# A fifth chunk of the exponentials off ScalarE, at pair 46, with the products on VectorE, and new orders of every engine, in a cosine-similarity attention kernel

## The chip, the cores and the metric

The kernel runs on one core of one Trainium2 chip. The metric is the device time of one execution in microseconds (us): the median over runs. A profile of one execution gives, beside its time, a trace of every instruction; "span" is the time from the first to the last instruction in that trace. Engines carry the profile's names: PE is TensorE (matmuls), PEld its weight loads, ACT ScalarE, DVE VectorE, POOL GpSimd, SP the engine that only issues transfers.

## The reference

For 8 batches of 12 heads, 512 rows of 64 numbers each:

```python
Q_norm = Q / (np.linalg.norm(Q, axis=-1, keepdims=True) + 1e-10)
K_norm = K / (np.linalg.norm(K, axis=-1, keepdims=True) + 1e-10)
scores = np.einsum('bhqd,bhkd->bhqk', Q_norm, K_norm) / tau
weights = np.exp(scores - np.max(scores, axis=-1, keepdims=True))
weights = weights / (np.sum(weights, axis=-1, keepdims=True) + 1e-10)
return np.einsum('bhqk,bhkd->bhqd', weights, V)
```

with tau = 0.1. Scores lie between -10 and 10, so the kernel subtracts no maximum.

## The kernel before, in words

**Pairs and chunks.** Two heads are a pair; there are 48 pairs, 0 to 47. The 512 keys of a pair are four chunks of 128. One chunk holds the scores of 128 keys against 512 queries for both heads: 128 x 1024 numbers. Every pair goes through the same stages, which the code names by short keys and this text uses as well:

- LD, LV (lines 340 to 344): transfers of Q, K and V from memory, issued by SP; ST (709) stores the output.
- SQ (lines 352 to 370): squares of Q and K on GpSimd. SSQ (397 to 411) and RED (382 to 424): their sums over 64 numbers, on TensorE and VectorE; for some pairs BN and RED (line 386) take Q's sums as batch statistics on VectorE.
- NEW (lines 446 to 478): the reciprocal roots of a group of up to four pairs, small steps on VectorE, held in the PSUM bank of `n_ps`. UNIT (481) rescales them for a pair that has a chunk off ScalarE.
- SCL (488 to 492): Q and K times their factors, Q on VectorE, K mostly on GpSimd. TR (497 to 505): transposes on TensorE into the bank `t_ps`. EVA (514 to 519): VectorE's copy of both transposes to SBUF.
- SCO (634 to 646): the scores of one chunk, two matmuls into one of two double banks of `sc_ps`; so a chunk's scores wait for the exponential of the chunk two before.
- EXP (654 to 662): ScalarE's exponential of a chunk, `et` in bfloat16. The last chunk of pair 47 is done in three pieces (647 to 653).
- VC (668 to 674): V cast to bfloat16 on GpSimd, mostly for two pairs at once.
- PV (678 to 694): weights times V, eight blocks of four matmuls for a pair. A column of ones beside V gives the row sums. RCP, NRM (702 to 708): reciprocal of the sums and the product, for both heads at once ("joint") or, in a pair with a chunk off ScalarE, for each head.

**A chunk off ScalarE.** `OFF` (line 755) lists chunks whose exponential is not ScalarE's: chunk 3 of pairs 26, 35, 41 and 46. `poly` (559 to 620) makes it from powers of two and a polynomial. For each head SCX puts the scores in the bank of the transposes (`x_ps` is the same memory as `t_ps`, line 157), after the copies of that pair; X0 (line 578) rounds them to an integer `xp` and X1 (580) takes the remainder `xz`, both on VectorE. Then GpSimd does five steps Y0 to Y4 over both heads (lines 600 to 607): square, scale, scale, product, product with the power of two. The blocks PV that use this chunk come last in their head and wait for Y4.

**The order of the work.** Nothing is decided at run time. Each engine executes its own list, written out in `ORDER` (lines 818 to 909) as numbers of operations in the order of `P.add`; an engine waits at an operation until all that it needs has been done, and everything behind it in its list waits as well. The lists interleave pairs: VectorE prepares pairs many places ahead of the one whose exponentials run. Decoded, VectorE's list ends, from the copy of pair 43 on (numbers are pair, head or tensor, step):

```
EVA.43 SCL.44.0 UNIT.46 SCL.45.0 SCL.46.0 EVA.44 RCP.40.0 NRM.40.0 EVA.45 EVA.46 RCP.41.0 X.46.0.0 NRM.41.0
X.46.0.1 RCP.41.1 NRM.41.1 X.46.1.0 X.46.1.1 RCP.42.0 NRM.42.0 SCL.47.0 RCP.43.0 NRM.43.0 RCP.44.0 NRM.44.0
EVA.47 RCP.45.0 NRM.45.0 RCP.46.0 RCP.46.1 NRM.46.0 NRM.46.1 RCP.47.0
...
```

GpSimd's ends `SQ.46 Y.41.0 Y.41.1 Y.41.2 Y.41.3 SCL.44.1 SCL.45.1 SCL.46.1 Y.41.4 VC.42 VC.44 VC.46 SCL.47.1 Y.46.0 Y.46.1 Y.46.2 Y.46.3 Y.46.4`.

## Time and profile before

| | us |
|---|---|
| median of 3 runs | 187.42 |
| lowest and highest run | 187.32, 188.6 |
| the profiled execution | 187.29 |
| its span | 185.3 |

How to read it: the busy time of an engine counts instructions that overlap once, so a mean duration times a count can exceed it. The chain that ended last is followed back from the last instruction, at each step to what released it; it is given as a list in order of time (start, length, what). A row of the groups has the line, engine and operation, the written and read tiles, the shape and the count, then total busy time and mean duration in ns, then the idle time of the engine in front of these instructions and who ended it. A timeline row has start, length, engine, line and operation, merged where several of a kind follow each other; an idle time in front stands in brackets. A row of waits has who waited for whom, the total, how often, and the longest.

### The profile page before, as it was taken

How to read it: one execution, taken by the hardware profiler on the slowest of the kernel's cores; microseconds unless marked ns; L12 is line 12 of the kernel's file. 1: busy time of each engine (PE TensorE's matmuls, PEld its weight loads, DVE VectorE, ACT ScalarE, POOL GpSimd, SP SyncE). 2: the span in 40 equal slices, each digit the busy share in tenths (PEclk: the TensorE clock that was granted, in tenths of full speed). 3: DMA queues.
4: the chain of work that ended last, by engine and by line, in shares of the span. 5: the costliest groups of instructions: out<-in, count | busy, mean ns of one | idle time of the engine just before them, and what ended most of it. 6: DMA issues, size and time to landing. Idle time of an engine off the chain costs nothing.

```text
span 185.3 us, 6949 instructions
## 1 busy us (share of the span) xinstructions
PE 174.9 (94%) x2802; PEld 111.4 (60%) x2802; DVE 167.6 (90%) x604; ACT 178.6 (96%) x208; POOL 162.2 (88%) x151
## 2 busy tenths in 40 slices
PE   7989999999999999999998999999899999899983
PEld 2556666666666666665664666675465656555652
DVE  2788999999999999999999999999999999989453
ACT  5799999999999999999999999999999999999993
POOL 4799989969889879696999999999899998999970
PEclk9999999999999999999999999999999999999998
DMA  5999999999999996999999996889978232211333
GB/s 172 343 351 350 350 358 339 283 340 377 379 379 382 371 372 217 278 371 355 379 363 357 381 378 217 233 263 316 357 252 265 79 117 79 96 61 57 117 113 117
DMA packets 52448, 50.79 MB, mean 274 GB/s; under 512 B 3136, under 2 KB 52416, under 8 KB 52416
## 3 DMA queue, kind: packets, MB, share of 16 engines
q1 hardware_dynamic: 51984, 50.02, 81.6%
q8 instruction: 22, 0.36, 0.8%
q10 hardware_dynamic: 432, 0.33, 0.5%
q14 instruction: 10, 0.08, 0.1%
HBM read 37.75 MB, written 12.58 MB: 272 GB/s over the span
## 4 chain that ended last, share of the span: by engine, by line
ACT 90%; PE 4%; DVE 2%; DMA 1%; issue 0%; POOL 0%; DVEq 0%
ACT et L660 89%; PE oops L685 2%; DMA qk<-in_K_dram 1%; PE scps L636 1%; DVE ob L706 1%; DVE xs L264 1%; PE oops L722 0%; DVE ob L735 0%; PE tps L287 0%; POOL sq L260 0%; ACT ys L437 0%; DVE qn L277 0%; PE scps L287 0%; DVE rd L704 0%; ACT nps L440 0%
## 5 line engine op out<-in xcount | busy, mean ns | idle before, releaser
L660 ACT ACTIVATE et<-scps 128x1024 bf16<-128x1024 f32 (+1 forms) x189 | 172.2, 1114 | 0.6 <-PE scps L636 0.5
L636 PE MATMUL scps<-qt 64*128 64x512 bf16 x376 | 73.9, 386 | 4.4 <-ACT et L660 2.8
L685 PE MATMUL oops<-vb,et 128*128 128x65 bf16 x1504 | 71.5, 194 | 0.6 <-DVE ob L706 0.3
L685 PEld LDWEIGHTS oops<-vb,et 128*128 128x128 bf16 x1504 | 54.8, 97 | 27.2 <-issue 19.3
L490 POOL TENSOR_TENSOR qn<-qk,rk 128x512 bf16<-128x512 f32 x42 | 43.3, 1043 | 8.7 <-DVE rk L448 7.2
L367 POOL TENSOR_TENSOR sq<-qk 128x512 bf16<-128x512 f32 x34 | 35.0, 1039 | 0.9 <-PE tps L499 0.8
L490 DVE TENSOR_TENSOR qn<-qk,nps 128x512 bf16<-128x512 f32 x52 | 34.4, 678 | 0.6 <-ACT nps L440 0.6
L706 DVE TENSOR_TENSOR ob<-oops,rd 128x512 f32<-128x512 f32 (+1 forms) x61 | 34.3, 563 | 0.2
L517 DVE COPY qt<-tps 128x1024 bf16<-128x1024 bf16 x47 | 32.2, 685 | 1.6 <-PE tps L499 1.1
L499 PE MATMUL tps<-ident,qn 128*128 128x128 bf16 x376 | 32.4, 220 | 1.0 <-DVE qn L490 0.6
L636 PEld LDWEIGHTS scps<-qt 64*128 64x128 bf16 x376 | 18.6, 92 | 22.0 <-ACT et L660 8.8
L386 DVE BATCH_NORM_STATS2 st<-qk 128x6 f32<-128x128 f32 x136 | 31.6, 284 | 0.0
L499 PEld LDWEIGHTS tps<-ident,qn 128*128 128x128 bf16 x376 | 21.4, 98 | 12.9 <-issue 8.0
L669 POOL TENSOR_SCALAR vb<-vf 128x1024 bf16<-128x1024 f32 (+1 forms) x29 | 25.9, 909 | 0.8 <-DMA vf<-in_V_dram 0.5
L370 POOL TENSOR_TENSOR sq<-qk 128x1024 bf16<-128x1024 f32 x10 | 18.8, 1893 | 0.3 <-DMA qk<-in_K_dram 0.3
L704 DVE RECIPROCAL rd<-oops 128x8 f32<-128x8 f32 (+1 forms) x61 | 11.6, 191 | 6.2 <-PE oops L685 5.1
L406 PE MATMUL oops<-sq,ident 128*128 128x64 bf16 x320 | 15.9, 193 | 0.0
L406 PEld LDWEIGHTS oops<-sq,ident 128*128 128x128 bf16 x320 | 12.0, 98 | 1.8 <-issue 1.4
L601 POOL TENSOR_TENSOR xw<-xw,xz 128x1024 f32<-128x1024 f32 x4 | 9.4, 2357 | 0.2
L601 POOL TENSOR_TENSOR xw<-xz 128x1024 f32<-128x1024 f32 x4 | 7.6, 1892 | 1.8 <-DVE xz L580 1.8
L601 POOL TENSOR_TENSOR et<-xw,xp 128x1024 bf16<-128x1024 f32 x4 | 8.5, 2130 | 0.2
L419 DVE TENSOR_REDUCE nps<-oops 128x8 f32<-128x64 f32 x36 | 7.4, 205 | 0.4 <-PE oops L406 0.2
(67 smaller groups left out, 102.8 us busy)
## 6 DMA issues: line engine op xcount, KB each, us to landing
vf<-in_V_dram SPq DMA_DIRECT2D x48, 256.0 KB, 6.5
qk<-in_Q_dram SPq DMA_DIRECT2D x47, 256.0 KB, 6.4
qk<-in_K_dram SPq DMA_DIRECT2D x47, 256.0 KB, 6.4
out_dram<-ob SPq DMA_DIRECT2D x47, 256.0 KB, 5.5
qk<-in_Q_dram SPq DMA_DIRECT2D x2, 128.0 KB, 2.4
qk<-in_K_dram ACTq DMA_DIRECT2D x2, 128.0 KB, 2.7
out_dram<-ob SPq DMA_DIRECT2D x1, 128.0 KB, 1.7
out_dram<-ob SPq DMA_DIRECT2D x1, 64.0 KB, 1.7
```

What stands on the lines that cost most here:

```text
L367: lambda e: e.tensor_tensor(out=sqf[:, 8 * DIM :], in0=data[:, 8 * DIM :], in1=data[:, 8 * DIM :], op=ALU.mult))
L386: last = e.bn_stats(out=st[:, g % R_X, c8 + 4 * h + t : c8 + 4 * h + t + 2, :].rearrange("p g x -> p (g x)"), in_=rows[:, t : t + 2].rearr ...
L406: last = e.matmul(out=o_ps[bank][:, at : at + 64], lhsT=ident[:, :], rhs=sq[iqs][:, 8 * w : 8 * w + 8, 8 * k : 8 * k + 8], start=(k == 0), ...
L490: lambda e, w=w, r=r: e.tensor_tensor(out=qn[iqn][:, w].rearrange("p t h d -> p h t d"), in0=qk[iq][:, w].rearrange("p h (t d) -> p h t d" ...
L499: last = e.transpose(t_ps[:, w, t, :], qn[iqn][:, w, t].rearrange("p h d -> p (h d)"), ident[:, :])
L517: lambda e, ws=ws: e.tensor_copy(out=qt[iqt][:, ws, :, :].rearrange("p w t x -> p (w t x)"), in_=t_ps[:, ws, :, :].rearrange("p w t x -> p ...
L601: mul = lambda o, x, y: lambda e: e.tensor_tensor(out=o, in0=x, in1=y, op=ALU.mult)
L636: last = e.matmul(out=sc_ps[:, 2 * b + h, :], lhsT=qt[iqt][64 * h : 64 * h + 64, 1, c, :], rhs=qt[iqt][64 * h : 64 * h + 64, 0, :, :], sta ...
L660: lambda e, c=c, b=b, hs=hs: e.activation(out=et[iet][:, c, hs[0] : hs[-1] + 1, :], in_=sc_ps[:, 2 * b + hs[0] : 2 * b + hs[-1] + 1, :], f ...
L669: return e.tensor_scalar(out=vb[:, ib // 2, :, ib % 2 : ib % 2 + n, :, 0:DIM].rearrange("p c r h d -> p (r h) c d"), in0=vf[:, iv : iv + n ...
L685: last = e.matmul(out=o_ps[h][:, 65 * t : 65 * t + 65], lhsT=et[iet][:, c, h, 128 * t : 128 * t + 128], rhs=vb[:, s % R_VB // 2, c, s % 2, ...
L706: lambda e, hs=hs, grid=grid: e.tensor_tensor(out=ob[io][:, hs], in0=grid[:, :, :, 0:DIM], in1=rd[io][:, hs, :].unsqueeze(3).to_broadcast( ...
```

## The change

Five chunks instead of four leave ScalarE: chunk 3 of pairs 25, 33, 40 and 44, done as before with five steps on GpSimd, and of pair 46, done in a new way (`IN_PSUM`). The scores of pair 46's chunk go to two banks: head 0 to the transposes' bank after the copy of pair 47 (the last that uses it), head 1 to the bank of the factors, after the scales of the last 12 pairs (`SCL`), when nothing uses it any more. X0 and X1 write tiles of their own (`yp`, `yz`). Then, for each head, VectorE makes the first product (Y1: `yz` and `yp`, both in SBUF, into the PSUM bank), GpSimd squares `yz` in place (Y2, after both Y1), and VectorE makes the second product (Y3: `yz` and the bank, into `et`). Y1 also waits for the last GpSimd step of pair 44. A constant factor that the products leave out is put into the other three chunks of pair 46: their exponentials get a bias, a tile of 128 x 1 that GpSimd sets once. The blocks PV of pair 46's chunk wait for Y3 of their own head alone. Pairs 26, 35 and 41 get joint normalisations; 25, 33, 40 and 44 get one for each head. `NRM_ON_POOL` is empty.

All six order lists are new. VectorE's, decoded, from the copy of pair 43 on:

```
EVA.43 SCL.44.0 NRM.39.0 EVA.44 SCL.45.0 UNIT.46 X.44.0.0 RCP.40.0 X.44.0.1 NRM.40.0 RCP.40.1 NRM.40.1 X.44.1.0
X.44.1.1 RCP.41.0 NRM.41.0 SCL.47.0 EVA.45 SCL.46.0 RCP.42.0 NRM.42.0 EVA.46 EVA.47 RCP.43.0 NRM.43.0 X.46.0.0
X.46.1.0 X.46.0.1 X.46.1.1 Y.46.0.1 RCP.44.1 RCP.44.0 NRM.44.1 NRM.44.0 Y.46.1.1 RCP.45.0 NRM.45.0 Y.46.0.3
Y.46.1.3 RCP.46.0 NRM.46.0 RCP.46.1 NRM.46.1 RCP.47.0
...
```

GpSimd's from the scale of pair 43 on: `SCL.43.1 Y.40.0 Y.40.1 Y.40.2 Y.40.3 SCL.44.1 Y.40.4 SCL.45.1 SCL.47.1 SCL.46.1 VC.44 Y.44.0 Y.44.1 Y.44.2 Y.44.3 Y.44.4 VC.46 Y.46.0.2 Y.46.1.2`; the cast VC.42 stands ahead of it, not behind. TensorE's has in the same stretch `SCO.42.2 PV.40.0.2 PV.40.0.3 PV.40.1.0 PV.40.1.1 PV.40.1.2 PV.40.1.3 SCO.42.3` and `SCO.45.0 TR.47.0 TR.47.1 PV.43.0.1 PV.43.1.2 PV.43.1.3 PV.43.0.2 PV.43.0.3 SCO.45.1 SCX.46.0 SCO.45.2 SCX.46.1`, and `SCO.46.2`, the eight PV of pair 45, `SCO.47.0` as before. The orders ahead of pair 24 differ mostly in places exchanged with a neighbour.

The diff without the order lists:

```diff
@@ -149,6 +149,10 @@
     xw = sb("xw", [128, 2, SEQ], f32)
+    if IN_PSUM:
+        yp = sb("yp", [128, 2, SEQ], mybir.dt.int16)
+        yz = sb("yz", [128, 2, SEQ], f32)
+        lift_in = sb("lift_in", [128, 1], f32)
 
@@ -157,7 +161,8 @@
            [sc_ps[:, 3 - h, 0 : SEQ // 2].bitcast(bf16).rearrange("p (t x) -> p t x", t=NT) for h in range(2)]]
-    n_ps = nc.alloc_psum_tensor("nps", [128, R_X, 160], f32)
+    nx_ps = nc.alloc_psum_tensor("nps", [128, SEQ], f32)[:, :]
+    n_ps = nx_ps[:, 0 : 160 * R_X].rearrange("p (x y) -> p x y", x=R_X)
 
@@ -191,6 +196,8 @@
     P.add("table", "act", "table", -900, [], lambda e: e.preload_act_table_set("natural_log_exp_and_others"))
+    if IN_PSUM:
+        P.add("lift", "pool", "sm_pool", 20, [], lambda e: e.memset(lift_in[:, :], -math.log(abs(POLY[3]) * 2.0 ** (127 - LIFT_K))))
     P.add("vone", "pool", "vone", -98, [], lambda e: e.memset(
@@ -560,38 +567,37 @@
         prev = [i for i in off_of if i < s]
+        held = [i for i in prev if not in_psum(i)]
         here = in_psum(s)
         a0, a1, a2, a4 = POLY
-        lift = LIFT_K if here else LIFT
         for h in range(2):
...
             before = [freed(*users[users.index((s, h)) - 1])] if users.index((s, h)) else []
-            if prev:
+            if turns[h] is None:
+                before += [("SCL", i, w) for i in range(NP - 12, NP) for w in range(2)]
+            elif prev:
                 before.append(freed(prev[-1], 1))
...
             def sco(e, h=h):
-                return e.matmul(out=x_ps, lhsT=qt[s % R_QT][64 * h : 64 * h + 64, 1, c, :],
+                return e.matmul(out=x_ps if turns[h] is not None else nx_ps, lhsT=qt[s % R_QT][64 * h : 64 * h + 64, 1, c, :],
                                 rhs=qt[s % R_QT][64 * h : 64 * h + 64, 0, :, :], start=True, stop=True)
 
-            P.add(("SCX", s, h), "pe", "sco1", at + h, [*evas(s), *evas(min(turns[h], last_eva))] + before, sco)
-            P.add(("X", s, h, 0), "pool" if s in X_ON_POOL else "dve", "x0" if s in X_ON_POOL else "x1", at + h, [("SCX", s, h)] + (exps(prev[-1], off_of[prev[-1]]) if prev else []),
-                  lambda e, h=h: e.tensor_scalar(out=xp[:, h, :], in0=x_ps, scalar1=BIG, scalar2=lift * UNIT - BIG, op0=ALU.add, op1=ALU.add))
+            P.add(("SCX", s, h), "pe", "sco1", at + h, [*evas(s), *evas(min(turns[0], last_eva))] + before, sco)
+            lift = LIFT_K if here else LIFT
+            b_ps = x_ps if turns[h] is not None else nx_ps
+            P.add(("X", s, h, 0), "dve", "x1", at + h, [("SCX", s, h)] + (exps(held[-1], off_of[held[-1]]) if held and not here else []),
+                  lambda e, h=h, b_ps=b_ps: e.tensor_scalar(out=(yp if here else xp)[:, h, :], in0=b_ps, scalar1=BIG, scalar2=lift * UNIT - BIG, op0=ALU.add, op1=ALU.add))
             P.add(("X", s, h, 1), "dve", "x1", at + h, [("X", s, h, 0)],
-                  lambda e, h=h: e.scalar_tensor_tensor(out=xz[:, h, :], in0=xp[:, h, :], scalar=a0 - lift * UNIT, in1=x_ps, op0=ALU.add, op1=ALU.subtract))
+                  (lambda e, h=h, b_ps=b_ps: e.scalar_tensor_tensor(out=yz[:, h, :], in0=b_ps, scalar=lift * UNIT - a0, in1=yp[:, h, :], op0=ALU.add, op1=ALU.subtract)) if here else
+                  (lambda e, h=h: e.scalar_tensor_tensor(out=xz[:, h, :], in0=xp[:, h, :], scalar=a0 - lift * UNIT, in1=x_ps, op0=ALU.add, op1=ALU.subtract)))
             if not here:
                 continue
-            p2 = xp[:, h, :].bitcast(bf16)
-            halves = [("pool", "yth", lambda e, h=h: e.tensor_tensor(out=x_ps, in0=xz[:, h, :], in1=xz[:, h, :], op=ALU.mult)),
-                      ("dve", "x1", lambda e, h=h, p2=p2: e.scalar_tensor_tensor(
-                          out=xw[:, h, :], in0=x_ps, scalar=a1, in1=p2, op0=ALU.add, op1=ALU.mult)),
-                      ("dve", "x1", lambda e, h=h: e.scalar_tensor_tensor(
-                          out=x_ps, in0=xz[:, h, :], scalar=a2, in1=x_ps, op0=ALU.mult, op1=ALU.add)),
-                      ("dve", "x1", lambda e, h=h: e.scalar_tensor_tensor(
-                          out=et[s % R_ET][:, c, h, :], in0=x_ps, scalar=a3, in1=xw[:, h, :], op0=ALU.add, op1=ALU.mult))]
-            for j, (eng, kind, step) in enumerate(halves):
-                P.add(("Y", s, h, j), eng, kind, at + 5 * h + 2 + 0.8 * j,
-                      [("Y", s, h, j - 1) if j else ("X", s, h, 1)]
-                      + ([key("PV", s - R_ET, i, NT - 1) for i in range(2)] if j == 3 else []), step)
+            halves = [lambda e, h=h, b_ps=b_ps: e.scalar_tensor_tensor(out=b_ps, in0=yz[:, h, :], scalar=-a2, in1=yp[:, h, :].bitcast(bf16), op0=ALU.add, op1=ALU.mult),
+                      lambda e, h=h: e.tensor_tensor(out=yz[:, h, :], in0=yz[:, h, :], in1=yz[:, h, :], op=ALU.mult),
+                      lambda e, h=h, b_ps=b_ps: e.scalar_tensor_tensor(out=et[s % R_ET][:, c, h, :], in0=yz[:, h, :], scalar=a1, in1=b_ps, op0=ALU.add, op1=ALU.mult)]
+            for j, (step, need) in enumerate(zip(halves, ([("X", s, h, 1)] + [("Y", i, 4) for i in held[-1:]], [("Y", s, i, 1) for i in range(2)],
+                                                          [("Y", s, h, 2)] + [key("PV", s - R_ET, i, NT - 1) for i in range(2)]))):
+                P.add(("Y", s, h, j + 1), "pool" if j == 1 else "dve", "sqp" if j == 1 else "x1", at + 2 + 0.5 * h + 0.8 * j, need, step)
         if here:
@@ -647,19 +653,19 @@
                     P.add(("EXP", s, c, k), "act", "exp1" if hi - lo == NT else "exph", T0 + 0.9 * c + 0.3 * k,
-                          [("SCO", s, c)] + [key("PV", s - R_ET, i, NT - 1) for i in range(2)],
+                          [("SCO", s, c)] + [key("PV", s - R_ET, i, NT - 1) for i in range(2)] + (["lift"] if in_psum(s) else []),
                           lambda e, c=c, b=b, h=h, q=slice(128 * lo, 128 * hi): e.activation(
-                              out=et[iet][:, c, h, q], in_=sc_ps[:, 2 * b + h, q], func=ACT.Exp, scale=math.log(2.0) / UNIT if s in off_of else inv_tau))
+                              out=et[iet][:, c, h, q], in_=sc_ps[:, 2 * b + h, q], func=ACT.Exp, scale=math.log(2.0) / UNIT if s in off_of else inv_tau, **({"bias": lift_in[:, :]} if in_psum(s) else {})))
                 continue
...
                       [("SCO", s, c) + hs if one and s == 0 else ("SCO", s, c)]
-                      + [key("PV", s - R_ET, h, NT - 1) for h in range(2)] + ["table"],
+                      + [key("PV", s - R_ET, h, NT - 1) for h in range(2)] + ["table"] + (["lift"] if in_psum(s) else []),
                       lambda e, c=c, b=b, hs=hs: e.activation(
                           out=et[iet][:, c, hs[0] : hs[-1] + 1, :], in_=sc_ps[:, 2 * b + hs[0] : 2 * b + hs[-1] + 1, :],
-                          func=ACT.Exp, scale=math.log(2.0) / UNIT if s in off_of else inv_tau))
+                          func=ACT.Exp, scale=math.log(2.0) / UNIT if s in off_of else inv_tau, **({"bias": lift_in[:, :]} if in_psum(s) else {})))
 
@@ -690,7 +696,7 @@
                 last_chunk = [c for c in range(NT) if c != off_of.get(s)] + [off_of.get(s)]
-                need, due = exps(s, last_chunk[i]) if s in off_of else sum((exps(s, c) for c in range(NT)), []), T0 + PERIOD + 0.9 * PV_AT[4 * h + i] + late(s)
+                need, due = ([("Y", s, h, 3)] if in_psum(s) and i == NT - 1 else exps(s, last_chunk[i])) if s in off_of else sum((exps(s, c) for c in range(NT)), []), T0 + PERIOD + 0.9 * PV_AT[4 * h + i] + late(s)
                 P.add(("PV", s, h, i), "pe", "pv", due, need + [cast_of(s)] + (bank_free[s, h] if i == 0 else [("PV", s, h, i - 1)]), pv)
@@ -702,7 +708,7 @@
                       lambda e, hs=slice(0, 2) if s in RCPJ else hs, grid=r_all: e.reciprocal(out=rd[io][:, hs, :], in_=grid[:, :, :, DIM]))
-            P.add(("NRM", s, h), "dve", "nrmj" if joint(s) else "nrm", T0 + PERIOD + 0.2 + 0.9 * PV_AT[4 * hh[-1] + 3] + late(s), [("RCP", s, 0 if s in RCPJ else h), key("ST", s - R_O)],
+            P.add(("NRM", s, h), "pool" if s in NRM_ON_POOL else "dve", "sclk" if s in NRM_ON_POOL else "nrmj" if joint(s) else "nrm", T0 + PERIOD + 0.2 + 0.9 * PV_AT[4 * hh[-1] + 3] + late(s), [("RCP", s, 0 if s in RCPJ else h), key("ST", s - R_O)],
                   lambda e, hs=hs, grid=grid: e.tensor_tensor(
@@ -725,7 +731,7 @@
                 op = P.add(("PV", s, k, c), "pe", "pv" if hi - lo == NT else "pvh", T0 + 0.9 * c + 2.5 + 0.1 * k,
-                           [("EXP", s, c, k) if c == NT - 1 else exps(s, c)[0], cast_of(s)]
+                           [("EXP", s, c, k) if c == NT - 1 else ("Y", s, h, 3) if in_psum(s) and (s, c) in OFF else exps(s, c)[0], cast_of(s)]
                            + ((evas(last_eva) + [freed(*u) for i in range(last_eva, NP) for u in turn_user.get(i, [])[-1:]] if k == 2 else bank_free[s, h]) if c == order[0] else [("PV", s, k, order[j - 1])]), pv)
@@ -751,8 +757,9 @@
 LIFT = 71
+LIFT_K = 102
 POLY = (-131.77899651091911, 109622.99404139613, -167.5284161360313, -2.6307902185888065e-08)
-OFF = {(26, 3): (26, 26), (35, 3): (35, 35), (41, 3): (41, 41), (46, 3): (46, 46)}
+OFF = {(25, 3): (25, 25), (33, 3): (33, 33), (40, 3): (40, 40), (44, 3): (44, 44), (46, 3): (47, None)}
 PIECES = ((0, 0, 4), (1, 0, 2), (1, 2, 4))
@@ -769,16 +776,16 @@
 STATS = (6, 8, 10, 12, 13, 14, 15, 16, 17, 18)
-IN_PSUM = ()
+IN_PSUM = (46,)
+NRM_ON_POOL = ()
 KAPPA = 157.0 / 128.0
-LIFT_K = 92
 POLY_K = (-50.88957745218819, 211913.74643901509, -543.4273783400707, 100350.14097237548, KAPPA * 2.0 ** -35)
...
 JOINT_FROM = 10
-OFF_ON_POOL = ((26, 3), (35, 3), (41, 3), (46, 3))
+OFF_ON_POOL = ((25, 3), (33, 3), (40, 3), (44, 3), (46, 3))
 OFF_ON_BOTH = ()
```

161 rows, old and new, of the table ORDER are left out of this document.

## Prediction

> **What bounds the kernel now.** I read the page first (busy shares, then the chain that ended last), then the busy time by stretch, then the chain in order of time.
>
> ```profile
> span 185.3 us, 6949 instructions
> PE 174.9 (94%) x2802; PEld 111.4 (60%) x2802; DVE 167.6 (90%) x604; ACT 178.6 (96%) x208; POOL 162.2 (88%) x151
> ACT 90%; PE 4%; DVE 2%; DMA 1%; issue 0%; POOL 0%; DVEq 0%
> L660 ACT ACTIVATE et<-scps 128x1024 bf16<-128x1024 f32 (+1 forms) x189 | 172.2, 1114 | 0.6 <-PE scps L636 0.5
> ```
> ```profile
> 24.00:165.00 141.00, 136.77 (x2237) 88.02 (x2232) 137.91 (x514) 140.98 (x155) 128.90 (x116) 1.00 0.88 292
> 165.00:182.00 17.00, 15.85 (x273) 10.06 (x270) 10.46 (x25) 16.85 (x21) 13.93 (x10) 1.00 0.29 94
> ```
> ```profile
> 11.81 113.70 ACT et L660 x124
> ...
> 125.53 45.95 ACT et L660 x50
> 171.48 0.05 issue
> 171.52 0.39 PE scps L636 x2
> 171.91 1.08 PE oops L685 x32
> 173.00 0.34 PE scps L636 x2
> 173.34 0.02 issue
> 173.36 2.87 ACT et L660 x3
> ...
> 180.52 0.43 DVE ob L706
> ```
>
> In the second fence the columns after the length are the busy times of PE, PEld, DVE, ACT and POOL. ScalarE's exponentials are the chain: from 24 to 165 us ScalarE is busy 140.98 of 141.00. But VectorE is busy 137.91 (3.1 idle) and GpSimd 128.90 (12.1 idle), so they have little to give before 165; after it VectorE idles 6.5 of 17 us. The price of an exponential on the path is its pitch, not its 1114 ns, for neighbours overlap: 113.70 / 124 = 0.917 us, and 45.95 / 50 = 0.919. The end is not pure ScalarE: from 171.48 the chain also passes TensorE and VectorE. The profiled execution took 187.29 us, its span and 2.0 around it; the median shown, 187.42, is 0.13 above it.
>
> **The change, part by part.**
>
> *One exponential fewer.* Five chunks instead of four leave ScalarE: -0.92 (row x124).
>
> *The bias of pair 46.* Its three remaining exponentials get a bias read from a tile. No exponential before shows one. The nearest rows are two small ScalarE functions of 128x16, the logarithm with a bias tile and the exponential without:
>
> ```profile
> L437 ACT ACTIVATE ys<-xs,eps 128x16 f32<-128x16 f32 x2 | 0.6, 312 | 0.0
> L440 ACT ACTIVATE nps<-ys 128x16 f32<-128x16 f32 x2 | 0.4, 188 | 0.1
> ```
>
> They differ by 124 ns, of which the function may be some. Three of them: 0 to 0.37; I take half, +0.19. The Trainium skill (ScalarE: Activation LUTs, the section that times ACTIVATE) gives about 93 ns for each pointer operand, an estimate of 0.28 for three; the sum by it would be 0.09 higher. The difference of the two rows does not contradict it. The memory set of that tile (128x1, once, on GpSimd) lies in a queue with 12.1 us to spare: nothing.
>
> *VectorE's work.* A chunk off ScalarE costs two passes for each of two heads; pair 46 costs two more for each head.
>
> ```profile
> L578 DVE TENSOR_SCALAR xp<-tps 128x512 int16<-128x512 f32 x8 | 5.5, 686 | 0.2 <-PE tps L573 0.2
> L580 DVE SCALAR_TENSOR_TENSOR xz<-xp,tps 128x512 f32<-128x512 int16 x8 | 5.5, 682 | 0.1
> 167.26 0.69 DVE L578 TENSOR_SCALAR xp<-tps 128x512 int16<-128x512 f32 x1 [0.16 <-PE tps L573]
> 167.87 0.41 DVE L706 TENSOR_TENSOR ob<-oops,rd 128x256 f32<-128x256 f32 x1
> ```
>
> A pass takes 0.68 but its neighbour starts 0.61 after it (167.26 to 167.87). Eight more passes are 4.9 us, all in the last stage by the new order (after the copy of pair 47's transposes). There VectorE idles 6.5, so it fits, if the passes fall into the gaps and not on the last chain. GpSimd loses one chunk of five steps at pair 46 but does one at 44: its whole extra is two squares of 128x512, below 1.04 each (a square of 128x1024 takes 1.89, below).
>
> *The middle: orders anew.* Chunks at 25, 33, 40 instead of 26, 35, 41 neither add nor remove work there; they move it. What it costs is the lead that the copies (L517) have over the scores that read them (L636). Pair 36 is a thin place:
>
> ```profile
> 134.85 0.88 DVE L386 BATCH_NORM_STATS2 st<-qk 128x6 f32<-128x128 f32 x4
> 137.12 0.68 DVE L517 COPY qt<-tps 128x1024 bf16<-128x1024 bf16 x1
> 137.71 0.68 DVE L490 TENSOR_TENSOR qn<-qk,nps 128x512 bf16<-128x512 f32 x1
> 138.61 0.39 PE L636 MATMUL scps<-qt 64*128 64x512 bf16 x2
> ```
>
> The copy ends at 137.80, its first score starts at 138.61: lead 0.81. Counting VectorE's order lists up to that copy, the new one has ahead of it, beyond the old: three jobs of statistics (0.88 / 2 = 0.44 each), the scale of pair 39 (0.6 by its 137.71 to 138.30 neighbour spacing), two small group steps and one more split of a normalisation: about 2.1 us. By itself that makes the score 2.1 - 0.81 = 1.3 late, less some 0.3 that a score has in hand before its exponential (two banks). Against it stand the 3.1 us that VectorE idled in this window: without those gaps it is on time. So 0 to 1.0.
>
> GpSimd says the same at pair 40. Before:
>
> ```profile
> 154.70 1.89 POOL L601 TENSOR_TENSOR xw<-xz 128x1024 f32<-128x1024 f32 x1 [0.60 <-DVE xz L580]
> 161.25 3.04 POOL L490 TENSOR_TENSOR qn<-qk,rk 128x512 bf16<-128x512 f32 x3
> 164.25 2.12 POOL L601 TENSOR_TENSOR et<-xw,xp 128x1024 bf16<-128x1024 f32 x1
> 162.35 0.39 PE L636 MATMUL scps<-qt 64*128 64x512 bf16 x2
> POOL qn L490 <- DVE rk L448: 7.2, 8, 1.5
> 87.71 3.04 POOL L490 TENSOR_TENSOR qn<-qk,rk 128x512 bf16<-128x512 f32 x3 [1.53 <-DVE rk L448]
> 88.80:154.70 65.90, 63.27 (x1012) 39.81 (x1009) 64.89 (x223) 65.88 (x74) 63.17 (x57) 1.00 0.84 276
> ```
>
> (Three timeline rows of GpSimd, one of TensorE, one of the waits, and busy times as above.) Pair 41's five steps took 154.70 to 166.37. Pair 40's have one K scale inside instead of three, so 11.67 - 2.0 = 9.7 us. In TensorE's new order the last score of pair 42 (before at 162.35; three exponentials are gone by then in both kernels) stands behind five output blocks of pair 40, 0.14 each (32 matmuls in 1.15, below), that need its fifth step. With 0.3 in hand that step must end by 162.35 + 0.3 - 0.7 = 161.9, so the first must start by 152.3, 2.4 earlier than pair 41's. GpSimd's queue ahead of it is longer by one cast (1.0). So 3.4 us of its 12.1 idle must go; 7.2 of these are waits for VectorE's group factors, which shrink only if VectorE comes earlier too. The last of them that is long ends with the scale of pair 24 at 87.71 (1.53). From there to 154.70 GpSimd idles 65.90 - 63.17 = 2.7. If all of that goes and the wait at 87.71 stays, the first step starts at 154.70 - 2.7 + 1.0 = 153.0, and the score is 0.7 late; if half of it stays, 2.1 late; if the wait at 87.71 shrinks too, it is on time. So 0 to 2.1, with the same cause as at pair 36, so not added to it. ScalarE's row of 140.98 of 141.00 shows queues as tight as this costing nothing, which is nearer to 0 than to 2.1: for both places together I take +0.3.
>
> *The last stage on TensorE.*
>
> ```profile
> 163.95 0.61 PE L499 MATMUL tps<-ident,qn 128*128 128x128 bf16 x8 [0.29 <-DVE rd L704]
> 171.84 1.15 PE L685 MATMUL oops<-vb,et 128*128 128x65 bf16 x32
> ```
>
> TensorE has 0.92 us for each chunk. Behind a score of the old pair 45 it has eight blocks: 171.52 to 173.00 is 1.48, 0.56 over. I take half of it as absorbed by the score that stands ready in the other bank and half, 0.28, as ScalarE's wait. The new order puts both transposes of pair 47 (0.61) and five blocks (5 x 0.14 = 0.72) behind the first score of pair 45 (0.34): 1.67, 0.75 over, wait 0.75 - 0.28 = 0.47. The eight blocks before pair 47 stand in both. So +0.19 (0 if the transposes fit, 0.47 if no wait of before goes).
>
> *The last stage on VectorE and GpSimd.* The first product of pair 46 waits for pair 44's fifth step, and behind it in VectorE's queue stand the normalisations of 44 to 47. If pair 40's steps end at 161.9, GpSimd still has three scales (3.04, above), a cast (3.10 / 3 = 1.03) and 44's five steps:
>
> ```profile
> 166.46 3.10 POOL L669 TENSOR_SCALAR vb<-vf 128x1024 bf16<-128x1024 f32 x3
> 170.91 1.89 POOL L601 TENSOR_TENSOR xw<-xz 128x1024 f32<-128x1024 f32 x1 [0.35 <-DVE xz L580]
> 177.58 2.12 POOL L601 TENSOR_TENSOR et<-xw,xp 128x1024 bf16<-128x1024 f32 x1
> ```
>
> 8.79 from 170.91 to 179.70, so 174.7. Then a product 0.61, two split normalisations 0.9, a product 0.65, two squares 2.1, a last product 0.65 and pair 46's first normalisation 0.65: 180.3, against 180.95 (180.52 + 0.43) before, a gain of 0.65. ScalarE's own gain is 0.92 - 0.19 - 0.19 = 0.54, so the products hide behind it: 0, with 0.1 in hand. From there every 1 us that pair 44's steps are late costs 1.
>
> On SP's queue loads and stores change places with a neighbour. The engine that takes loads first is GpSimd, whose casts waited for one by 0.5 in all:
>
> ```profile
> L669 POOL TENSOR_SCALAR vb<-vf 128x1024 bf16<-128x1024 f32 (+1 forms) x29 | 25.9, 909 | 0.8 <-DMA vf<-in_V_dram 0.5
> ```
>
> Nothing, then, and up to 0.5 if such a wait comes once more at a place without cover.
>
> Sum: -0.92 + 0.19 + 0.3 + 0.19 = -0.24 on 187.29, so 187.05; plus 0.13 for the median, **187.2 us**.
>
> **Rivals.**
>
> *The middle waits (slower).* VectorE's and GpSimd's idle time recurs in the new order. Half of GpSimd's 2.7 stays and the score at pair 40 is 1.5 to 2.1 late instead of 0.3: 187.2 + 1.2 = 188.4, up to 189.0. For it: 7.2 us of GpSimd's waits end on VectorE, which has only 3.1 of idle itself. Against: ScalarE has not waited so far. It decides once pair 40's first step starts after about 152.6.
>
> *A two-input product stands behind GpSimd.* Pair 46's first products read two tiles of SBUF; each VectorE group that I list reads at most one, with PSUM as the other input (L580, L706, L490). If such a pass had to wait for the GpSimd instruction in flight, it would meet the last cast, which GpSimd starts when pair 44's steps end: 1.0 us of delay, less 0.1 in hand, so 188.1. The Trainium skill (SBUF — State Buffer, Who interferes with whom) speaks for this: a VectorE instruction with two SBUF inputs and a GpSimd instruction that reads SBUF exclude each other for a whole instruction. No row here has such a pair, so the trace cannot say.
>
> *All of the gain.* The bias is hidden, the middle costs nothing, and TensorE's slot is no worse: 187.42 - 0.92 = 186.5, and 186.2 if the 0.28 wait at 173.36 goes too.
>
> **How the numbers follow.** The small gain (186.7 to 187.8) 0.50; the middle waits 0.22; the two-input product 0.10; all of the gain 0.18. A measurement of this kernel can tell about 1%, 1.87 us, from no change: below 185.55 nothing reaches by these terms (0.03 for what I don't see), above 189.29 only the middle waits or the two-input product with something besides (0.09); within, 0.88. The range 186.2 to 188.9 leaves out about 0.15.
>
> **What would show it.** Right: 188 exponentials on the line that has 189, ScalarE with next to no wait up to pair 45, one wait of about 0.5 behind pair 47's transposes, 20 instead of 16 first passes on VectorE, pair 44's last GpSimd step near 175. Wrong: ScalarE's pitch broken at pairs 28, 36 or 42 with the copy L517 or pair 40's fifth step as the last to come; products of pair 46 far over 0.68; a first normalisation of pair 46 after 181.

## The result and the profile after

| | before | after |
|---|---|---|
| median of 14 runs each, us | 187.45 | 188.95 |
| lowest and highest run | 187.16, 190.04 | 188.09, 190.46 |
| the profiled execution | 187.29 | 188.18 |
| its span | 185.3 | 186.2 |

The ratio of after to before is 1.0077, interval 1.0056 to 1.0098: a loss of 0.6 to 1.0% where the prediction had a small gain, to 187.2 us, and the median lies just above its range. The profiled execution is near the lowest of the 14 runs; its 0.89 us over the one of before can be traced instruction by instruction, the rest of the 1.50 between the medians cannot. Five of the 14 executions after had a granted clock of 0.982 to 0.991 and took 189.18 to 190.46 us; the other nine, at 0.997 or more, have a median of 188.40, 0.95 above that of all runs before.

The page after: span, busy shares, the chain by engine, and the exponentials' own group.

```profile
span 186.2 us, 6956 instructions
...
PE 172.8 (93%) x2802; PEld 110.7 (59%) x2802; DVE 173.4 (93%) x615; ACT 178.2 (96%) x207; POOL 164.1 (88%) x154
...
ACT 69%; PE 20%; POOL 4%; DVE 2%; issue 2%; DMA 1%; POOLq 1%; DVEq 0%
...
L666 ACT ACTIVATE et<-scps 128x1024 bf16<-128x1024 f32 (+1 forms) x185 | 168.9, 1109 | 1.8 <-PE scps L642 1.6
```

The 185 exponentials, and three with a bias that the trace lists apart, are the 188 that were announced. But they wait 1.8 us instead of 0.6, and GpSimd, with 0% of the old chain, holds 4% of the new one. Where it does is at the end of the chain in order of time (start, length, what):

```profile
170.57 2.35 POOL xw L607
173.00 2.13 POOL et L607
175.21 1.06 POOL vb L675
176.26 2.07 issue
178.33 1.08 POOLq L87
179.41 1.01 POOL yz L596
180.44 0.69 DVE et L597
181.37 0.44 DVE ob L712
```

The end now goes through pair 44's last two GpSimd steps, the last cast of V, the squares of pair 46 and its last product. The busy times by stretch (PE, PEld, DVE, ACT, POOL) answer to the two rows of before, the second stretch being 1 us longer:

```profile
24.00:165.00 141.00, 136.11 (x2240) 87.91 (x2238) 138.80 (x518) 140.79 (x154) 132.18 (x120) 1.00 0.87 292
165.00:183.00 18.00, 15.16 (x272) 10.14 (x270) 15.47 (x32) 16.67 (x20) 12.80 (x10) 1.00 0.27 89
```

Up to 165 us ScalarE is nearly as full as before (0.19 less); GpSimd has taken on 3.3 us. After 165 VectorE is busy 15.47 instead of 10.46 (4.9 more were expected), and ScalarE idles 1.33. The timelines of that stage, VectorE, GpSimd, ScalarE and TensorE in turn:

```profile
175.23 1.58 DVE L595 SCALAR_TENSOR_TENSOR tps<-yz,yp 128x512 f32<-128x512 f32 x1 [0.18 <-POOL et L607]
176.72 0.24 DVE L710 RECIPROCAL rd<-oops 128x4 f32<-128x4 f32 x2
176.93 0.76 DVE L712 TENSOR_TENSOR ob<-oops,rd 128x256 f32<-128x256 f32 x2
177.60 0.69 DVE L595 SCALAR_TENSOR_TENSOR nps<-yz,yp 128x512 f32<-128x512 f32 x1
...
179.44 0.69 DVE L597 SCALAR_TENSOR_TENSOR et<-yz,tps 128x512 bf16<-128x512 f32 x1
```
```profile
173.00 2.13 POOL L607 TENSOR_TENSOR et<-xw,xp 128x1024 bf16<-128x1024 f32 x1
175.21 1.06 POOL L675 TENSOR_SCALAR vb<-vf 128x1024 bf16<-128x1024 f32 x1
178.37 2.04 POOL L596 TENSOR_TENSOR yz<-yz 128x512 f32<-128x512 f32 x2 [2.11 <-DVE nps L595]
```
```profile
174.77 3.13 ACT L666 ACTIVATE et<-scps,lift_in 128x1024 bf16<-128x1024 f32 x3
178.92 1.94 ACT L666 ACTIVATE et<-scps 128x1024 bf16<-128x1024 f32 x2 [1.02 <-PE scps L642]
```
```profile
177.41 1.15 PE L691 MATMUL oops<-vb,et 128*128 128x65 bf16 x32 [1.06 <-DVE ob L712]
178.49 0.61 PE L642 MATMUL scps<-qt 64*128 64x512 bf16 x4
```

The reader is to see four links. The first product of pair 46 starts 0.02 us after the cast on GpSimd and takes 1.58, its twin 2.4 us later takes 0.69; it ends at 176.81, 0.54 after the cast (175.21 + 1.06 = 176.27). The two normalisations of pair 44 stand behind it on VectorE. Pair 45's 32 matmuls wait for them (1.06), since they need the bank that they empty. Pair 47's first score stands behind those on TensorE, and its exponential waits 1.02.

A ledger for the comparisons below is worked out from the starts of all exponentials: *path*, from the first of pair 1 to the end of the last one; *extra*, the sum of what their spacing has above 0.904, the spacing where the queue is full, counted where it is 0.04 or more; *pair 47*, the part of that before its first exponential; *tail*, from the end of the last exponential to the end of the last normalisation.

| | path | extra | pair 47 | tail | path + tail |
|---|---|---|---|---|---|
| before | 169.38 | 2.31 | 0.24 | 1.07 | 170.45 |
| after | 170.19 | 4.05 | 1.25 | 1.22 | 171.41 |
| cast_waits | 169.33 | 3.11 | 0.38 | 1.41 | 170.74 |
| memset_for_cast | 169.35 | 3.13 | 0.39 | 1.21 | 170.56 |
| four_chunks | 169.76 | 2.53 | 0 | 1.80 | 171.56 |
| four_chunks_b | 169.73 | 2.62 | 0 | 1.08 | 170.81 |
| te_order | 170.80 | 4.41 | 1.07 | 1.21 | 172.01 |
| no_bias | 169.30 | 3.16 | 0.55 | 1.40 | 170.70 |
| cast_moved | 169.61 | 3.46 | 0.69 | 1.13 | 170.74 |
| orders_early | 169.44 | 3.44 | 0.36 | 1.41 | 170.85 |
| cast44_on_dve | 169.35 | 3.09 | 0.39 | 1.42 | 170.77 |
| cast44_no_bias | 169.42 | 3.21 | 0.57 | 1.41 | 170.83 |
| x44_early | 170.70 | 4.51 | 0.52 | 1.41 | 172.11 |

After against before: one spacing less (-0.90), 1.74 more extra, of which 1.01 is before pair 47, and 0.15 in the tail.

### The profile page after: what moved, and what is told of

Its sections match the earlier page's. It is cut to its first block, busy times and chain, and to the rows that moved or that the text cites. A ratio compares the mean times of both kernels' runs of the same rounds, so it can differ in the third digit from the quotient of the medians.

```text
span 186.2 us, 6956 instructions
## 1 busy us (share of the span) xinstructions
PE 172.8 (93%) x2802; PEld 110.7 (59%) x2802; DVE 173.4 (93%) x615; ACT 178.2 (96%) x207; POOL 164.1 (88%) x154
## 4 chain that ended last, share of the span: by engine, by line
ACT 69%; PE 20%; POOL 4%; DVE 2%; issue 2%; DMA 1%; POOLq 1%; DVEq 0%
ACT et L666 68%; PE scps L642 7%; PE oops L691 7%; PE tps L506 3%; DMA qk<-in_K_dram 1%; POOL xw L607 1%; POOL et L607 1%; PE oops L413 1%; PE oops L408 1%; POOLq L87 1%; DVE xs L271 1%; POOL vb L675 1%; POOL yz L596 1%; PE oops L728 0%; DVE qt L305 0%
## 5 line engine op out<-in xcount | busy, mean ns | idle before, releaser
L666 ACT ACTIVATE et<-scps 128x1024 bf16<-128x1024 f32 (+1 forms) x185 | 168.9, 1109 | 1.8 <-PE scps L642 1.6
L691 PE MATMUL oops<-vb,et 128*128 128x65 bf16 x1504 | 70.1, 194 | 2.1 <-DVE ob L712 1.9
L506 PE MATMUL tps<-ident,qn 128*128 128x128 bf16 x376 | 33.0, 221 | 0.7 <-DVE qn L497 0.6
```

The costliest lines, as they stand in the source:

```text
L506: last = e.transpose(t_ps[:, w, t, :], qn[iqn][:, w, t].rearrange("p h d -> p (h d)"), ident[:, :])
L666: lambda e, c=c, b=b, hs=hs: e.activation(out=et[iet][:, c, hs[0] : hs[-1] + 1, :], in_=sc_ps[:, 2 * b + hs[0] : 2 * b + hs[-1] + 1, :], f ...
L691: last = e.matmul(out=o_ps[h][:, 65 * t : 65 * t + 65], lhsT=et[iet][:, c, h, 128 * t : 128 * t + 128], rhs=vb[:, s % R_VB // 2, c, s % 2, ...
```

## The experiments

The theory after the result: the first product of pair 46 and GpSimd's cast exclude each other; that puts pair 47 and the end 0.9 us back. Rivals: the new orders alone cost it (in the middle or on TensorE), or the product is long for a reason of its own.

**cast_waits**: the cast waits for the first product.

```diff
-... for i in range(n) for h in range(2)] + ["vone"], cast)
+... for i in range(n) for h in range(2)] + ["vone"] + ([("Y", 46, 0, 1)] if s == 46 else []), cast)
```

> The last cast of V (pairs 46 and 47) waits for pair 46's first product instead of running beside it; nothing else differs from the changed kernel. Theory 1 (the two-input product and GpSimd's cast exclude each other, and the normalisations of pair 44 behind the product hold up TensorE): the first product takes 0.69 instead of 1.58 us, the normalisation of pair 44 ends 0.9 earlier, ScalarE's wait before pair 47 shrinks from 1.25 to about 0.35, the end comes about 0.75 earlier: 188.2 us, ratio to before 1.004. The cast itself, or the second product, is then late by up to 0.3. Rival (the product is slow because of the bank it writes or the wait for pair 44's step, and the new orders in the middle set the time): the product still takes about 1.6 and the time stays at 188.9.

Measured: 187.62 us, ratio to before 1.0011 (0.9999 to 1.0023). The durations came as the theory had them, the time lower than its 188.2. VectorE and GpSimd:

```profile
175.24 0.70 DVE L595 SCALAR_TENSOR_TENSOR tps<-yz,yp 128x512 f32<-128x512 f32 x1 [0.19 <-POOL et L607]
...
176.73 1.00 DVE L595 SCALAR_TENSOR_TENSOR nps<-yz,yp 128x512 f32<-128x512 f32 x1
```
```profile
176.13 1.06 POOL L675 TENSOR_SCALAR vb<-vf 128x1024 bf16<-128x1024 f32 x1 [0.99 <-DVE rd L710]
```

The first product is back at 0.70. The second now meets the cast, in flight for 0.60 us when it starts, and takes 1.00. The wait before pair 47 falls from 1.25 to 0.38. The median gains more (1.33) than the profiled executions (188.18 to 187.56).

**memset_for_cast**: in place of the last cast GpSimd sets a tile of its own to a constant, so the cast of V for pairs 46 and 47 is left out.

```diff
+    junk = sb("junk", [128, 1024], f32)
...
 def cast(e):
+    if s == 46:
+        return e.memset(junk[:, :], 1.0)
```

> In place of the last cast GpSimd writes a constant into a tile of its own, 128x1024 of float32: it reads nothing of SBUF. Left out: the cast of V for pairs 46 and 47, which use older values of V. Theory 1, in the form that only GpSimd instructions that read SBUF exclude the product: the first product takes 0.69 us beside it. Theory 1 in a wider form (any GpSimd instruction): the product ends about 0.5 after the constant's end. Rival (the product is slow by itself): 1.6 us.

One execution, 187.75 us. GpSimd and VectorE, from the timelines:

```profile
175.61 0.95 POOL L677 MEMSET junk<- 128x1024 f32 x1
```
```profile
175.77 0.70 DVE L596 SCALAR_TENSOR_TENSOR tps<-yz,yp 128x512 f32<-128x512 f32 x1 [0.21 <-POOL et L608]
```

A GpSimd instruction of about the same length at the same place, started 0.16 us ahead of the product, that only writes SBUF: the product takes 0.70. So its length in the changed kernel is neither its bank's nor its operands' own. What the memory set lacks beside the cast is the reading; that the tile it writes plays no part is seen in lock_long, where a GpSimd instruction that reads SBUF and writes a tile of the same kind collides. By the ledger the whole price of the cast is 0.85 (171.41 - 170.56).

**lock_long**: a further GpSimd product of two SBUF tiles (its output unused), to stand beside VectorE's second product.

```diff
+if s == 46:
+    P.add(("JUNK", 46), "pool", "yt", T0, [("Y", 46, 0, 1), ("NRM", 44, 0)], lambda e: e.tensor_tensor(
+        out=junk[:, :], in0=xz[...], in1=xz[...], op=ALU.mult))
```

> The changed kernel with one further GpSimd product of two tiles in SBUF (1.9 us, its output is not used) started together with VectorE's second product, behind the same normalisation. Theory (a VectorE product of two operands from SBUF stands aside for a GpSimd instruction that reads SBUF, for as long as that one lasts): the second product takes 1.9 to 2.6 us instead of 0.69. Rival (the first product is long for another reason, as its bank or its inputs): 0.7 us. The time itself says little, since the squares queue behind the added product on GpSimd: 189 to 190 by either.

One execution, 190.74 us, at a mean clock of 0.99 (0.78 from 176 to 180 us, where 32 matmuls take 1.94 instead of 1.15). The expectation missed: the second product took 0.69, because VectorE came first, by 0.16 us. GpSimd's product is the one that is long (VectorE's timeline, then GpSimd's):

```profile
176.20 1.58 DVE L596 SCALAR_TENSOR_TENSOR tps<-yz,yp 128x512 f32<-128x512 f32 x1 [0.21 <-POOL et L608]
...
178.58 0.69 DVE L596 SCALAR_TENSOR_TENSOR nps<-yz,yp 128x512 f32<-128x512 f32 x1
```
```profile
167.29 1.90 POOL L608 TENSOR_TENSOR xw<-xz 128x1024 f32<-128x1024 f32 x1
...
178.74 2.27 POOL L683 TENSOR_TENSOR junk<-xz 128x1024 f32<-128x1024 f32 x1 [1.50 <-DVE ob L716]
```

2.27 against 1.90 for the same form without company. The lower clock is not the reason, for GpSimd's two squares right behind it take 2.03, in the changed kernel 2.04. The one that starts second stands aside. The first product meets the cast as in the changed kernel and takes the same 1.58.

**four_chunks and four_chunks_b**: the new orders, but pair 46's fourth chunk back on ScalarE. With no chunk off ScalarE pair 46 gets a joint normalisation by the rule of `joint`; four_chunks leaves it so, and four_chunks_b keeps two (the last changed line), with pair 46's blocks by heads in TensorE's list.

```diff
-OFF = {(25, 3): (25, 25), (33, 3): (33, 33), (40, 3): (40, 40), (44, 3): (44, 44), (46, 3): (47, None)}
-IN_PSUM = (46,)
+OFF = {(25, 3): (25, 25), (33, 3): (33, 33), (40, 3): (40, 40), (44, 3): (44, 44)}
+IN_PSUM = ()
...
-return JOINT and s >= JOINT_FROM and s not in {i for i, _ in OFF} and s < 47
+return JOINT and s >= JOINT_FROM and s not in {i for i, _ in OFF} and s < 46
```

> The new orders with the fifth chunk put back on ScalarE: chunks 25, 33, 40, 44 only; pair 46's last chunk has its scores behind three of pair 45's blocks and its exponential on ScalarE, and nothing of the new way is left. Theory 1 with the middle as seen in the trace (some 0.45 us of ScalarE waits at pairs 15, 28, 36 and 42 that the old orders don't have): 187.45 + 0.45 + 0.05 for pair 47's transposes = 187.9 us, ratio 1.0025. Rival A (all of the loss comes with the fifth chunk): 187.45, ratio 1.000. Rival B (all of it comes with the orders): 188.9, ratio 1.008.

> The changed kernel's orders and its four earlier pairs, but pair 46's fourth chunk is left on ScalarE (no products, squares or bias), and pair 46 keeps its two normalisations, each as soon as its head's four blocks are done, so that the last blocks don't wait as they did in four_chunks. What this measures is the new orders by themselves. Theory (the new orders cost ScalarE's path 0.38 us, as four_chunks' records showed, and nothing behind it): about 187.8 us, ratio to before 1.002. Rival A (the new orders cost nothing, the whole loss came from the fifth chunk): 187.45, ratio 1.000. Rival B (the tail of four_chunks was no artefact of the joint normalisation): 188.6, ratio 1.006.

Measured: four_chunks 188.67 us, ratio 1.0062 (1.0047 to 1.0077); four_chunks_b 187.76, ratio 1.0019 (1.0005 to 1.0032). The first is spoilt at its end, as its chain shows: pair 47's blocks stand behind the joint normalisation of pair 46, and the tail is 1.80.

```profile
181.94 0.70 DVE ob L712
183.04 0.44 PE oops L728 x14
183.73 0.42 DVE ob L741
```

The second has the tail of before and no wait before pair 47; its path is 0.35 longer. So the new orders alone cost 0.35 us. That is a balance: new waits, 0.36 instead of 0.14 before pair 15's first exponential (ahead of any chunk off ScalarE) and 0.28, 0.41 and 0.21 at pairs 28, 36 and 42, against waits of before that are gone, 0.24 before pair 47 among them. Against it, cast_waits says what a fifth chunk brings once the products meet no cast at first: path 0.40 less, tail 0.33 more. Of the 0.90, 0.07 is left.

**te_order**: four exchanges in TensorE's list that bring a late score ahead (the edit in words, for the list itself is numbers).

```
 SCO.28.0: SSQ.34.1 behind it
 SCO.36.0: PV.34.0.2, PV.34.0.3, SSQ.42.1 behind it
 SCO.42.3: PV.40.1.1 to PV.40.1.3 behind it
 SCO.45.1: the five PV of pair 43 behind it
```

> The changed kernel with four places of TensorE's list exchanged, so that scores stand ahead of work that is not urgent: the sums of pair 34 behind the first scores of 28, two output blocks of 34 and the sums of 42 behind the first scores of 36, three blocks of pair 40 behind the last scores of 42, five blocks of 43 behind the second scores of 45. Theory 1: ScalarE's waits at these places shrink by about 0.23, 0.3, 0.2 and 0.3, but pair 47 still stands behind pair 44's normalisation, which follows GpSimd's steps and not ScalarE, so the wait before pair 47 grows by as much and the time stays at 188.9 us, at most 0.2 less. Rival (the middle sets the time): about 1.0 less, 187.9 us, ratio 1.0025.

Measured: 189.02 us, ratio 1.0081 (1.0064 to 1.0097). Pair 36's first exponential no longer waits (extra 0.41 to 0.05), its third does (0.52); pair 45's second is on time (0.34 to under 0.05), its fourth is not (0.52). What TensorE is spared at one place it lacks two chunks on. The time is Theory 1's, but not for its reason: the wait before pair 47 did not grow (1.07 against 1.25), the middle did. The first product meets the cast here too and takes 1.50.

**orders_early**: cast_waits with the order of before up to pair 19's first exponential on every engine.

> cast_waits with the order of before up to the first exponential of pair 19 on every engine, and the new order from there. Theory (0.22 us of the middle's loss lies at pair 15, ahead of any of the chunks, and is a matter of the orders alone): the wait before pair 15's first exponential falls from 0.36 to 0.14 us over the pitch, and the end comes 0.2 us earlier: 187.4. Rival (what is won there is lost at the next place where TensorE is behind, as with te_order): 187.6.

Measured: 187.88 us, ratio 1.0036 (1.0018 to 1.0054), no better than cast_waits. The extra before pair 15 falls from 0.36 to 0.14 as expected, and that before pair 20's third exponential grows from 0.21 to 0.42. The rival held.

**no_bias**: cast_waits without the bias; pair 46's polynomial is fitted anew with the leading factor -2^-25, so that the other chunks need no factor.

```diff
-        a0, a1, a2, a4 = POLY
+        a0, a1, a2, a4 = POLY_UNIT if here else POLY
...
-func=ACT.Exp, scale=..., **({"bias": lift_in[:, :]} if in_psum(s) else {})))
+func=ACT.Exp, scale=...))
```

> cast_waits (the last cast waits for the first product) with the bias operand of pair 46's three exponentials gone: the polynomial of pair 46 is fitted anew with a leading factor that is a power of two, so that no rescaling of the other chunks is needed. Theory (the bias operand costs 0.09 us each): pair 46's second and third exponentials follow at 0.90 us instead of 1.00. By the prediction's term that is 0.2 us off the end, 187.4. Rival (pair 47 stands behind pair 44's normalisation, which stands behind GpSimd's last step, and not behind pair 46's exponentials): the pitch falls, the wait before pair 47's first exponential grows by the same 0.2 us, and the time stays at 187.6. Second rival (the pitch of 1.00 is no cost of the bias): the pitch stays.

Measured: 187.58 us, ratio 1.0004 (0.9984 to 1.0024). The spacing of pair 46's second and third exponentials falls from 1.00 to 0.90, and the extra before pair 47 grows from 0.38 to 0.55: the first rival. The bias costs ScalarE 0.09 for each of the two and the end nothing, because pair 47 stands behind pair 44's normalisation.

**cast_moved**: the last cast on VectorE, ahead of pair 47's copy; the first square waits for its own product alone.

```diff
-P.add(("VC", s), "pool", ...
+P.add(("VC", s), "dve" if s == 46 else "pool", ...
-[("Y", s, i, 1) for i in range(2)],
+[("Y", s, i, 1) for i in range(h + 1)],
```

> The changed kernel with the last cast of V taken from GpSimd to VectorE, ahead of pair 47's copy of the transposes, where VectorE was idle for 1.0 us; the first square waits for its own product alone. Theory (the first product is long because GpSimd's cast stands beside it, and the tail hangs on GpSimd's queue): the first product takes 0.70 us, the wait before pair 47's first exponential is about 0.4 us, and pair 46's last product comes some 1 us earlier than in cast_waits, so that its normalisation no longer holds pair 47's blocks; the tail is 0.3 us shorter: 187.2 to 187.3. Rival A (the end hangs on ScalarE's path alone): like cast_waits, 187.6. Rival B (VectorE's cast is itself held up beside GpSimd's steps): a cast of 2 us or more, pair 47's copy later, 188 or more.

Measured: 187.86 us, ratio 1.0046 (1.0014 to 1.0078). The tail is short (1.13) as the theory had it, but the wait before pair 47 is 0.69. VectorE's cast and GpSimd's fourth step of pair 44:

```profile
170.27 0.99 DVE L675 TENSOR_SCALAR vb<-vf 128x1024 bf16<-128x1024 f32 x1
```
```profile
170.80 2.67 POOL L607 TENSOR_TENSOR xw<-xw,xz 128x1024 f32<-128x1024 f32 x1
```

The step takes 2.67 instead of 2.35 (chain of after). The cast itself takes 0.99, having started while GpSimd's third step ran; without company it takes 0.69 (cast44_on_dve). The collision has moved from the product to the step that everything waits for: rival B, in a small form.

**cast44_on_dve and cast44_no_bias**: cast_waits with the cast of pairs 44 and 45 on VectorE instead; the second also without the bias.

> cast_waits with the cast of V of pairs 44 and 45 taken from GpSimd to VectorE, into the 1.0 us in which VectorE was idle ahead of pair 47's copy; the last cast stays on GpSimd behind the first product. Theory (the end hangs on GpSimd's dense queue up to pair 44's last step): GpSimd is rid of 1.06 us ahead of pair 44's five steps and gives back some 0.3 us where its fourth step meets VectorE's cast, as in cast_moved; pair 44's last step ends 0.7 us earlier, the wait before pair 47's first exponential falls from 0.38 us to under 0.15, the tail behind the last exponential from 1.41 to 1.1: 187.0. Rival A (pair 47 stands behind TensorE's order as before, not behind pair 44's last step): the wait stays near 0.3, 187.4. Rival B (VectorE's cast costs elsewhere what it saves): 187.6.

> cast44_on_dve and no_bias together. Theory: the bias counts once pair 47 no longer stands behind pair 44's normalisation, so this is 0.1 to 0.2 us below cast44_on_dve, about 186.8, ratio to before 0.997, faster than both kernels. Rival: the same as cast44_on_dve, because pair 47's first exponential is again what waits.

Measured: 187.84 us, ratio 1.0027 (1.0003 to 1.0050), and 187.99, ratio 1.0022 (0.9993 to 1.0050). The theory missed: the wait before pair 47 is 0.39 and the tail 1.42, as in cast_waits. GpSimd, in cast44_on_dve:

```profile
166.19 1.89 POOL L607 TENSOR_TENSOR xw<-xz 128x1024 f32<-128x1024 f32 x1 [0.80 <-DVE xz L592]
...
170.43 2.67 POOL L607 TENSOR_TENSOR xw<-xw,xz 128x1024 f32<-128x1024 f32 x1
```

Of the 1.06 us that it was rid of, it waits 0.80 for VectorE's passes of pair 44 and loses 0.32 to VectorE's cast.

**x44_early**: cast44_no_bias with these passes drawn ahead on VectorE, and TensorE's list around them.

> cast44_no_bias with pair 44's rounding passes drawn together on VectorE (ahead of the second half of pair 40's normalisation), its second score product ahead of pair 43's first scores on TensorE, and pair 41's blocks and pair 45's transposes put around them. In cast44_on_dve and cast44_no_bias GpSimd was rid of the cast and then waited 0.8 us for these passes. Theory (the end hangs on pair 44's last GpSimd step, and that on VectorE's passes): GpSimd's first step of pair 44 starts about 0.5 us earlier against the exponentials, the wait before pair 47's first exponential falls from 0.57 to about 0.1 us, and the tail from 1.4 to 1.1: about 0.7 us less than cast44_no_bias's records, 186.8, ratio to before 0.997. Rival (what moves here makes TensorE late at pairs 43 to 45): the steps come earlier, but ScalarE waits 0.3 us or more at a score of these pairs, and the time stays at 187.4 or goes above.

Measured: 189.10 us, ratio 1.0100 (1.0083 to 1.0117). The rival, and more of it than it said; ScalarE's waits for scores, from the waits of the whole span (total, times, longest):

```profile
ACT et L666 <- PE scps L642: 1.9, 5, 0.6
```

Counted from pair 42's first exponential, GpSimd's first step of pair 44 starts 0.26 earlier than in cast44_no_bias, but scores of pairs 43 to 45 come late by 0.17 to 0.58. No version here is faster than before: cast_waits, no_bias and cast44_no_bias can't be told from it, and the intervals of the others lie above 1.

## Why the prediction was wrong

*The step that failed* is the last stage on VectorE and GpSimd, which ended "so the products hide behind it: 0, with 0.1 in hand". It measured 1.01 before pair 47 and 0.15 in the tail. Two things were wrong in it, and two of the prediction's signs of being wrong came true: a product far over 0.68, and a first normalisation of pair 46 after 181.

It took a product at 0.61, its spacing beside PSUM-fed neighbours. The rival "a two-input product stands behind GpSimd" is what happened, at its place (the last cast) and close to its price: the products' delay of "1.0 us" is 1.58 - 0.70 = 0.88. That it got 0.10 of the chance was a misjudgement: no row of before had such a pair, so the trace was silent, while the one source that spoke was for it. The Trainium skill (SBUF — State Buffer, Who interferes with whom) says that a VectorE instruction with two SBUF inputs and a GpSimd instruction that reads SBUF exclude each other, that one that only writes does not take part, and that whoever issues first goes first. The runs agree on each: 1.58 behind the cast, 0.70 beside the memory set, and GpSimd's 2.27 instead of 1.90 where VectorE was first.

And it followed the products along one chain only, to pair 46's normalisation and the end: 180.3, against 181.81 for the end of that normalisation in the chain (181.37 + 0.44). It had named the normalisations of 44 to 47 as queued behind the product, but not who waits for that of pair 44: pair 45's blocks, and behind these on TensorE pair 47's first score. cast_waits shows this chain without the collision at the first product: the extra before pair 47 is 0.38 even then, against 0 in four_chunks_b.

*One exponential fewer*, -0.92: measured -0.90 (spacing 0.904).

*The bias*, +0.19: 0.09 for each of the two spacings that show it, 0.18. The Trainium skill (ScalarE: Activation LUTs, the section that times ACTIVATE) gives about 93 ns for a pointer operand; the measured 0.09 agrees. But it stood beside the wait for pair 44's normalisation, where it costs the end nothing (no_bias).

*The middle and TensorE's slot*, +0.3 and +0.19: four_chunks_b measures both together at 0.35. The size was near, but by luck, for the mechanism was another. The argument asked how late VectorE's copies and GpSimd's steps would come. ScalarE's new waits at pairs 28, 36 and 42 end behind TensorE's own list, which it counted for pairs 45 and 47 alone. At pair 36 (extra 0.41) the copy is done at 138.91, and the score still stands behind six blocks and the sums of pair 42, without idle time on TensorE (VectorE's row, then TensorE's):

```profile
138.22 0.69 DVE L524 COPY qt<-tps 128x1024 bf16<-128x1024 bf16 x1
138.20 0.90 PE L691 MATMUL oops<-vb,et 128*128 128x65 bf16 x24
138.94 0.40 PE L413 MATMUL oops<-sq,ident 128*128 128x64 bf16 x8
139.27 0.39 PE L642 MATMUL scps<-qt 64*128 64x512 bf16 x2
```

At pair 40 GpSimd came nearly as the prediction asked, with a start at 152.55 against 152.3, and the score of pair 42 behind it is 0.21 late. But the steps are not what it waits for:

```profile
152.55 1.89 POOL L607 TENSOR_TENSOR xw<-xz 128x1024 f32<-128x1024 f32 x1
...
160.10 2.13 POOL L607 TENSOR_TENSOR et<-xw,xp 128x1024 bf16<-128x1024 f32 x1
161.86 0.49 PE L642 MATMUL scps<-qt 64*128 64x512 bf16 x2
162.29 0.90 PE L691 MATMUL oops<-vb,et 128*128 128x65 bf16 x24
163.12 0.39 PE L642 MATMUL scps<-qt 64*128 64x512 bf16 x2
```

The fifth step ends at 162.23, while TensorE is still at the score before; the six blocks then run without a wait. They need 0.84 (0.14 each), and beside a score (0.34) the spacing of 0.904 leaves 0.56. te_order, with three of them behind the score, has no wait there. At pair 15 orders_early shows the orders as the cause; the argument never looked there. The rival that the middle waits for 1.2 us and more did not happen. For TensorE's slot at pair 45 the extra is 0.34 instead of 0.28: +0.06, not +0.19.

*Pair 44's last step* was put at 174.7 and ended at 173.00 + 2.13 = 175.13; that 0.4 adds to what pair 47 waits for.

So the gain of 0.90 went to: the orders 0.35, the bias 0.18, the wait for pair 44's normalisation and the longer tail (0.38 and 0.33 in cast_waits), and the collision at the first product took another 0.67 (171.41 - 170.74). That is 1.91, against 1.86 by the ledger (0.90 + 0.96). What stays open: the changed kernel's median lies 0.77 above its profiled execution, where that of cast_waits lies 0.06 above its own. The lower clock of five executions goes with 0.55 of it (188.95 - 188.40), and none of the twelve of cast_waits had one below 0.995; whether the change brings it about is not shown. The collision itself came alike in two more traces, lock_long and te_order: 1.58 and 1.50.

## What to carry to other kernels

Before a new kind of instruction is put on an engine, list what the other engines have in flight at that moment; when no row shows the pair, the price is open, and a rule that gives one deserves more than a token chance. Follow everything queued behind a late instruction to the engine that sets the time, through the queues of the engines between, not only the chain that the change was made for. When orders change, count what each engine has to do between two urgent instructions, TensorE too. In this kernel, with four engines at 88% and more, a gain on one came back as a wait elsewhere: te_order, orders_early, cast44_on_dve and x44_early each moved a wait and removed none.

## What the runs showed of the hardware

The price of a collision is regular in these traces: the one that comes second is longer by what is left of the first when it starts, less 0.14 to 0.16 us. Product behind cast: 1.04 left, 0.88 longer (after); 0.46 left (176.13 + 1.06 - 176.73 = 0.46), 0.30 longer (cast_waits). GpSimd behind VectorE's product: 178.58 + 0.69 - 178.74 = 0.53 left, 0.37 longer (lock_long). VectorE's cast, with one operand in SBUF, also collides, both ways (cast_moved): behind GpSimd's third step it takes 0.99 instead of 0.69, and 170.27 + 0.99 - 170.80 = 0.46 of it is left when the fourth starts, which is 0.32 longer. A product with one SBUF operand and one in PSUM does not: 0.69 at 179.44, inside GpSimd's squares (178.37 to 180.41).
